# Last products through six PSUM accumulators, and modulation units moved to the ends of mixers and norms

## Chip, cores and metric

One Trainium2 chip, of which the kernel uses one core. The metric is the device time of one execution in microseconds (us). TensorE is called PE, VectorE DVE, ScalarE ACT, GpSimd POOL; SP issues nearly all DMAs, in order.

## What is computed

Two transformer blocks in a row on 256 latent tokens of width 1024, with 256 context tokens beside them, all in float32. The first block has two layers. Each splits one projection into three mixers, joins their outputs in one product, and has a feed-forward with a convolution; the context goes through layer 0 as well, but not through the end of layer 1. Every sum into x is gated by a modulation vector, which is itself a product of the condition c with a large weight:

```python
sh1, sc1, g1, sh2, sc2, g2 = modulation(c, w_ada[i], b_ada[i])
h = modulate(rms_norm(x, norm1_g[i]), sh1, sc1)
a_z, bq, bk, bv, cq, ck, cv = split_proj(h @ w_in[i])
...
x = x + g1 * (jnp.concatenate([out_a, out_b, out_c], axis=-1) @ w_out[i])
x = x + g2 * conv_ffn(modulate(rms_norm(x, norm2_g[i]), sh2, sc2),
                      w_up[i], conv_w[i], conv_b[i], w_down[i])
```

out_a is a gated MLP over positions, out_b windowed attention with grouped heads and a sink, out_c differential attention whose result gets a norm of its own. The second block has one layer with full attention and one with a pooling mixer, each with such a feed-forward.

## The kernel before

**Products.** A float32 product is made of three faster ones. `mms` issues them: high part by high part (L285), low part of the activations by high part of the weights or the like (L286), high by low (L289). The weights come through a staging tile `w`; ACT casts the high half (wh, L238) and DVE subtracts for the low half (wl, L240). Activations are cast on ACT (hH, mixH, gH) and their rest made on DVE or POOL (hL, mixL, gL). One product of 256 columns over four tiles of 128 rows is 12 matmuls.

**PSUM.** The products named `acc` use two buffers of one bank, transposes and small sums `tr` two, scores and the feed-forwards' `up` products `S` two buffers of two banks each. Where a buffer is free only when DVE or ACT has read it, PE waits.

**Order.** The orders of PE and SP are those of the code. Those of ACT, DVE and POOL are set by a scheduler. The class `Line` runs the pieces of work as generators: each yields a cost and a waiting time (table WAIT), and `Line` goes on with a piece when its estimated due time has come, so pieces are interleaved on PE's order. `spread(main, fill)` puts the elements of one list evenly between those of another.

**Mixer.** `block1` builds the list `seq`: the chunks of the projection (c0 to c7 of the latent and context stream), the score groups of the three mixers (`b_unit`: scores on PE at L807 with a mask at L810, maximum on DVE at L661, exponentials on ACT at L817; `c_unit`: the like, with products L873 and L881 for its own norm and a cast to mixH at L266), and the first half of the output product, `wouts(0)`. In layer 1 a table of four moves, `MOVES`, then takes elements at given places of `seq` to other places, counted modulo its length. Behind `seq` come, stream by stream, the last eight output products, `wouts(1)` (`wout`, residual at L980, sums of squares, and the norm's products at L485 and L486).

**Feed-forward.** `ffn` makes `up` products, and `down` products in groups; those of the last group stand at its end, eight per stream, each with its residual (L980) or, in the second block, its sum into y (L1051). Behind them come the next norm (var, rstd, and per tile ht at L529 and hL at L540) and the next layer's first chunk.

**Modulation units.** A unit loads a piece of the modulation weight (`mod_load`, on SP: `mw` in two halves through three buffers, or `wm` of 1 MB through the larger pool x8), multiplies (L410), adds up on ACT or DVE (L414, L416) and now and then transposes (L426). Each unit loads for the next one. `fill_a` gives layer 0 its 16 pieces, 12 elements between the scores and five between the first output products; layer 1 has eight pieces spread over `seq` from its twelfth element on.

Of the kernel before, what the change touches and what calls it, by code (L numbers as in the profile page):

```python
# [19 lines left out]
P = 128  # L20
# [59 lines left out]
def spread(main, fill):  # L80

    out, done = [], 0
    for i, u in enumerate(main):
        out.append(u)
        want = len(fill) * (i + 1) // len(main)
        out += fill[done:want]
        done = want
    return out + fill[done:]
# [17 lines left out]
class Stack:  # L106
# [191 lines left out]

    def psum(self, tag, shape):
        return self.ps.tile(shape, F32, tag=tag, name=tag)  # L300

    def x8(self, name, dt=F32):
        return self.xp.tile([P, CH], dt, tag="x8", name=name)
# [402 lines left out]
    def block1(self, l, after):  # L706
# [12 lines left out]
        u, gk = uv[:, 0], f"gn{l}"  # L719
# [5 lines left out]
        def mix_tiles(g):  # L725
            if g not in mix:
                if f"wout{l}" in WHOLE:
                    t = self.gp.tile([P, CH], F32, tag="gH", name="mix") if g == 0 else self.x8("mix")
                    mix[g] = (t.rearrange("p (k t) -> p k t", k=4),)
                elif g == 0:  # L730
                    mix[g] = (self.gp.tile([P, 4, 512], F32R, tag="gH", name="mixH"),
                              self.gp.tile([P, 4, 512], F32R, tag="gL", name="mixL"))
                else:
                    mix[g] = tuple(self.x8(t, F32R).rearrange("p (k t) -> p k t", k=4) for t in ("mixH", "mixL"))
            return mix[g]

        def chunk(ci, post, ss):
            return [lambda s=s: self.go(self.proj(f"win{l}", ci, s, post), f"c{ci}{s}") for s in ss]
# [6 lines left out]
        def post_bq(c):  # L745
            return lambda acc, s: self.qk(acc, 4, 64, tbq, self.sm(gk, "bq"), s == 0, rsB[:, s, :, c], 2,
                                          qTB[:, s, 2 * c:2 * c + 2])
# [142 lines left out]
        def wout(g, cc, f4, c):  # L890

            m = mix_tiles(g)
            w = self.weights(f"wout{l}", 2 * g + cc, k=4)
            ft = 4 * cc + f4
            acc = self.psum("acc", [P, 512])
            fs = slice(P * f4, P * f4 + P)
            yield from self.mms([acc[:, c]], range(4), lambda b, k: [x[:, k, fs] for x in w],
                     lambda b, k: [x[:, k, c] for x in m])
            self.residual(l, 2, acc, ft, [q for q in streams if c.start <= 256 * q < c.stop])
            if g == 1:  # L900
                self.sumsq(nst[c.start // 256], self.xs[c.start // 256][:, ft], ft == KD - 1)

        def wouts(g, c):
            return [lambda cc=cc, f4=f4: self.go(wout(g, cc, f4, c)) for cc in range(2) for f4 in range(4)]
# [18 lines left out]
        need = lambda *names: [lambda: line.ensure(*names)]  # L923
        rev = streams[::-1]
        fill = self.fill_a(l)
        seq = chunk(0, post_bkv, (0,)) + chunk(1, post_bq(0), (0,)) + chunk(0, post_bkv, (1,))
        if l == 0:
            seq += chunk(1, post_bq(0), (1,))
        else:
            seq = seq[:2] + need("n1") + [self.last_loads] + seq[2:]  # L930
        self.qk_wait = WAIT[f"qk{l}_first"]
        seq += [lambda: setattr(self, "qk_wait", WAIT[f"qk{l}"])]
        heavy = (chunk(2, post_bq(1), streams) + chunk(3, post_ck, both) + chunk(4, post_cq, streams)
# [18 lines left out]
        for a, b in MOVES[l]:  # L952
            seq.insert((a + b) % len(seq), seq.pop(a % len(seq)))
        if l == 1:
            seq = seq[:12] + spread(seq[12:], self.more_units((1, 12, 20)))
        for u_ in seq:
            u_()
        if l == 1:
# [1 line left out]
            self.ctx2_h()  # L960
        for q in streams:
            line.ensure(*(f"c_{hp}{q}11" for hp in range(2)))
            for u_ in wouts(1, slice(256 * q, 256 * q + 256)):
                u_()
            line.due()
            self.go(self.norm_h(l, 3, self.sm(key, "n2g"), nst[q], q), f"n{q}")
# [29 lines left out]
    def ffn(self, i, T, streams, after):  # L996


        nc, key = self.nc, f"sm{i}"
        post = i >= 2  # L1000
        groups = FF_GROUPS[T]
        starts = [sum(groups[:g]) for g in range(len(groups))]
        nst = {q: {} for q in streams}
        y = self.x8("y").rearrange("p (k t) -> p k t", k=KD) if post else None
        gt = {}
        cols = 512 if T == 512 else 256

        def up(g, j):
            a = j - starts[g]
            if a == 0:  # L1010
                gt[g] = tuple(self.gp.tile([P, groups[g], T], F32R, tag=t, name=t) for t in ("gH", "gL"))
            wh, wl = self.weights(f"wup{i}", j, k=KD)
            ps = self.psum("S", [P, 2, 512])
            for q in streams:
                hH, hL = self.h[q]
                yield from self.mms([ps[:, b, 256 * q:256 * q + 256] for b in range(2)], range(KD),
                         lambda b, k: (wh[:, k, P * b:P * b + P], wl[:, k, P * b:P * b + P]),
                         lambda b, k: (hH[:, k], hL[:, k]))
            c = self.pt.tile([P, 2, 512], F32, tag="pt", name="cgv")
            self.conv(c[:, 0, :T], ps[:, 0, :T], key, j)  # L1020
            nc.scalar.activation(c[:, 0, :T], c[:, 0, :T], AF.Silu)
            if i < 2:
                self.conv(c[:, 1, :T], ps[:, 1, :T], key, KF + j)
                nc.vector.tensor_tensor(c[:, 1, :T], c[:, 0, :T], c[:, 1, :T], ALU.mult)
            else:
                nc.vector.tensor_tensor(c[:, 1, :T], c[:, 0, :T], ps[:, 1, :T], ALU.mult)
            gH, gL = gt[g]
            nc.scalar.copy(gH[:, a], c[:, 1, :T])  # L1028
            (nc.vector if T == 512 else nc.gpsimd).tensor_tensor(gL[:, a], c[:, 1, :T], gH[:, a].bitcast(F32), ALU.subtract)  # L1029
            if j == KF - 1:  # L1030
                self.lnexp()

        def down(g, ft, c):
            gk = groups[g]
            cc, f4 = divmod(ft, cols // P)
            wh, wl = self.weights(f"wdn{i}", g, cc, k=gk)
            gH, gL = gt[g]
            fs = slice(P * f4, P * f4 + P)
            acc = self.psum("acc", [P, 512])
            yield from self.mms([acc[:, c]], range(gk), lambda b, k: (wh[:, k, fs], wl[:, k, fs]),  # L1040
                     lambda b, k: (gH[:, k, c], gL[:, k, c]))
            last = g == len(groups) - 1
            if not post:
                self.residual(i, 5, acc, ft, [q for q in streams if c.start <= 256 * q < c.stop])
                if last:
                    self.sumsq(nst[c.start // 256], self.xs[c.start // 256][:, ft], ft == KD - 1)
            else:
                if g == 0:
                    nc.scalar.copy(y[:, ft], acc[:, :256])
                else:  # L1050
                    nc.vector.tensor_tensor(y[:, ft], y[:, ft], acc[:, :256], ALU.add)  # L1051
                if last:
                    self.post_sums(nst[0], y[:, ft], ft, i == 3)

        main = []
        for kind, g, j in self.ffn_order(T):
            if kind == "up":
                main.append(lambda g=g, j=j: self.go(up(g, j)))
            elif g < len(groups) - 1:
                main += [lambda g=g, ft=ft: self.go(down(g, ft, slice(0, T))) for ft in range(KD)]  # L1060
        for u in spread(main, self.fill_f(i)):
            u()
        if i == 0:
            self.prep1(1)
        if post:
            nst[0] = self.post_start(i, 5, self.sm(key, "post2"))
        for q in streams:
            for ft in range(KD):
                self.go(down(len(groups) - 1, ft, slice(256 * q, 256 * q + 256)))
                if i == 2:  # L1070
                    self.early_loads(ft)
            after(q, nst[q], y)
# [260 lines left out]
    def fill_a(self, l):  # L1333

        if l:
            return [], []
        u = self.more_units((0, 8, 24))
        return u[:12], u[12:]

    def fill_f(self, i):  # L1340

# [78 lines left out]
    def first(self, S, wh, wl, pr, s):  # L1420
        mm = self.nc.tensor.matmul
        hH, hL = self.h[s]
        for k in (2 * pr, 2 * pr + 1):
            for t in range(2):
                o, ts = S[:, t, :256], slice(P * t, P * t + P)
                mm(o, lhsT=hH[:, k, ts], rhs=wh[:, k], start=k == 0, stop=False)
                mm(o, lhsT=hH[:, k, ts], rhs=wl[:, k], start=False, stop=False)
                mm(o, lhsT=hL[:, k, ts], rhs=wh[:, k], start=False, stop=k == KD - 1)
# [197 lines left out]
```

## Time and profile before

| | us |
|---|---|
| median of three runs | 1756.46 |
| the runs | 1751.83, 1756.46, 1756.65 |
| the profiled execution's own time | 1754.48 |
| its span, first to last instruction | 1752.7 |
| PE busy in it | 1599.5 |
| DVE busy in it | 1188.5 |

PE's mean granted clock is 0.967 of full speed. In the profile an instruction's line is that of the kernel; `out<-in` are the tiles. A wait is the idle time of an engine before an instruction, with what released it. The places by time: layer 0's first output products lie from 205 to 266 us, the last ones up to 312; the first feed-forward ends at 741, where layer 1 begins; its mixer goes on to 920; the third feed-forward ends near 1490.

### The profile page before, as it was taken

Reading aid. Unit: us, or ns where it says so; the run is one execution under the profiler, and the core shown is the slowest. Engines: PE = TensorE matmul, PEld = TensorE weight load, DVE = VectorE, ACT = ScalarE, POOL = GpSimd, SP = SyncE. Lnnn points to the kernel's source line nnn. Section 1 sums busy time; section 2 is a strip of 40 time slices with the busy share of each in tenths; the row PEclk is TensorE's granted clock in tenths of the full one; section 3 lists DMA queues with packets and bytes.
Section 4 is the critical chain, followed back from the end, with each engine's and each line's share of the span. In section 5 each row is a group of like instructions: output and inputs, shape, how many; then the busy total and the mean of one; then the engine's idle time right before and its main releaser. Section 6 shows DMA issues by size and latency. Waiting matters only on the chain.

```text
span 1752.7 us, 32334 instructions
## 1 busy us (share of the span) xinstructions
PE 1599.5 (91%) x12604; PEld 1419.1 (81%) x12604; DVE 1188.5 (68%) x2877; ACT 879.1 (50%) x2147; POOL 136.7 (8%) x162
## 2 busy tenths in 40 slices
PE   6999797999999999889888998988979999779997
PEld 5877457989898989788468998976869999479996
DVE  5765886755555545777788777785776567876665
ACT  6344654523242324455546656563556555656563
POOL 1000001000000000010000101000141012330110
PEclk9999998999999999999899999999989999889999
DMA  8344330444545454334334544565554546435552
GB/s 326 107 145 145 125 125 32 146 182 177 219 143 217 168 205 176 131 119 154 133 109 151 195 167 139 175 220 208 197 180 164 196 155 226 174 118 196 170 176 88
DMA packets 67402, 288.36 MB, mean 165 GB/s; under 512 B 7728, under 2 KB 9008, under 8 KB 54960
## 3 DMA queue, kind: packets, MB, share of 16 engines
q1 hardware_dynamic: 65664, 283.91, 46.0%
q10 hardware_dynamic: 1584, 2.38, 0.4%
q8 instruction: 99, 1.62, 0.4%
q14 instruction: 55, 0.45, 0.1%
HBM read 285.21 MB, written 1.05 MB: 163 GB/s over the span
## 4 chain that ended last, share of the span: by engine, by line
PE 61%; DVE 18%; DMA 10%; ACT 7%; issue 3%; POOL 1%; SPq 0%; ACTq 0%; DVEq 0%; POOLq 0%
PE S L285 9%; PE S L286 9%; PE S L289 9%; PE acc L285 8%; PE acc L286 8%; PE acc L289 8%; DVE wl L240 6%; DMA w<-in_wup_dram 5%; PE acc L410 3%; ACT wh L238 2%; DMA w<-in_wdn_dram 2%; DVE ht L529 1%; PE tr L671 1%; DMA wm<-in_wmod_dram 1%; DVE mx L661 1%
## 5 line engine op out<-in xcount | busy, mean ns | idle before, releaser
L240 DVE TENSOR_TENSOR wl<-w,wh 128x384 fp32r<-128x384 f32 (+2 forms) x1010 | 489.1, 523 | 218.5 <-ACT wh L238 190.7
L238 ACT CAST wh<-w 128x384 fp32r<-128x384 f32 (+2 forms) x1010 | 421.3, 475 | 329.4 <-DMA w<-in_wup_dram 94.9
L285 PE MATMUL S<-hH,wh 128*128 128x256 f32 x1408 | 351.3, 287 | 31.0 <-ACT hH L539 17.4
L286 PE MATMUL S<-hL,wh 128*128 128x256 f32 x1408 | 349.2, 285 | 4.7 <-POOL hL L537 4.0
L285 PEld LDWEIGHTS S<-hH,wh 128*128 128x128 f32 x1408 | 271.6, 193 | 36.9 <-ACT hH L539 18.1
L286 PEld LDWEIGHTS S<-hL,wh 128*128 128x128 f32 x1408 | 271.5, 193 | 7.1 <-POOL hL L537 5.0
L285 PE MATMUL acc<-gH,wh 128*128 128x256 f32 (+1 forms) x728 | 209.0, 311 | 9.2 <-DVE xc L980 4.8
L286 PE MATMUL acc<-gL,wh 128*128 128x256 f32 (+1 forms) x728 | 205.3, 306 | 0.0
L289 PE MATMUL S<-hH,wl 128*128 128x256 f32 x1408 | 198.4, 284 | 0.0
L289 PEld LDWEIGHTS S<-hH,wl 128*128 128x128 f32 x1408 | 182.6, 193 | 0.0
L285 PEld LDWEIGHTS acc<-gH,wh 128*128 128x128 f32 x728 | 138.9, 191 | 23.6 <-issue 7.0
L289 PE MATMUL acc<-gH,wl 128*128 128x256 f32 (+1 forms) x728 | 145.7, 306 | 0.0
L286 PEld LDWEIGHTS acc<-gL,wh 128*128 128x128 f32 x728 | 138.9, 191 | 5.5
L991 DVE SCALAR_TENSOR_TENSOR cgv<-S,sm,cgv 128x255 f32<-128x255 f32 (+1 forms) x132 | 74.8, 567 | 67.6 <-ACT cgv L988 67.1
L289 PEld LDWEIGHTS acc<-gH,wl 128*128 128x128 f32 x728 | 110.2, 191 | 6.5
L988 ACT ACTIVATE cgv<-S,sm 128x256 f32<-128x256 f32 (+1 forms) x132 | 82.7, 628 | 47.3 <-PE S L289 47.3
L285 PE MATMUL acc<-wh,hH 128*128 128x256 f32 x344 | 91.2, 296 | 10.4 <-ACT hH L539 8.2
L1029 POOL TENSOR_TENSOR gL<-cgv,gH 128x256 fp32r<-128x256 f32 x66 | 52.2, 791 | 579.5 <-ACT gH L1028 558.7
L980 DVE SCALAR_TENSOR_TENSOR x<-acc,mod,x 128x256 f32<-128x256 f32 x104 | 50.0, 482 | 57.7 <-PE acc L289 57.3
L286 PE MATMUL acc<-wl,hH 128*128 128x256 f32 x344 | 88.1, 287 | 0.0
L286 PE MATMUL S<-hcL,wh 128*128 128x256 f32 x352 | 86.5, 284 | 0.3 <-DVE hcL L540 0.3
L285 PE MATMUL S<-hcH,wh 128*128 128x256 f32 x352 | 86.4, 280 | 0.0
(268 smaller groups left out, 2837.4 us busy)
## 6 DMA issues: line engine op xcount, KB each, us to landing
wm<-in_wmod_dram SPq DMA_DIRECT2D x72, 1024.0 KB, 7.6
w<-in_wup_dram SPq DMA_DIRECT2D x140, 512.0 KB, 3.9
w<-in_wdn_dram SPq DMA_DIRECT2D x56, 512.0 KB, 4.1
mw<-in_wmod_dram SPq DMA_DIRECT2D x48, 512.0 KB, 4.7
w<-in_wup_dram SPq DMA_DIRECT2D x18, 1024.0 KB, 7.5
w<-in_win_dram SPq DMA_DIRECT2D x32, 512.0 KB, 4.0
w<-in_wout_dram SPq DMA_DIRECT2D x16, 512.0 KB, 4.7
w<-in_wqkv_dram SPq DMA_DIRECT2D x16, 512.0 KB, 3.9
```

The lines of the kernel that those rows point to most:

```text
L238: self.nc.scalar.copy(h[:, c:d], w[:, c - a:d - a])
L240: self.nc.vector.tensor_tensor(l[:, c:d], w[:, c - a:d - a], h[:, c:d].bitcast(F32), ALU.subtract)
L285: mm(o, lhsT=s[0], rhs=m[0], start=k == ks[0], stop=False)
L286: mm(o, lhsT=s[0], rhs=m[1], start=False, stop=False)
L289: mm(o, lhsT=S(b, k)[1], rhs=M(b, k)[0], start=False, stop=end and k == ks[-1])
L410: nc.tensor.matmul(acc[32 * u:32 * u + 32], lhsT=self.cpad[:, k], rhs=w[:, 256 * u:256 * u + 256], start=k == ks[0], stop=k == ks[-1])
L529: nc.vector.scalar_tensor_tensor(t, self.xs[s][:, ft], A, r, ALU.mult, ALU.mult)
L661: nc.vector.tensor_reduce(mx, S[:, :, :nk], AX.X, ALU.max)
L980: self.nc.vector.scalar_tensor_tensor(x, acc[:, c], self.mods(i, j)[:, ft, s:s + 1], x, ALU.mult, ALU.add)
L988: nc.scalar.activation(out, ps, AF.Identity, scale=cw[:, n + f:n + f + 1], bias=cb[:, f:f + 1])
L991: nc.vector.scalar_tensor_tensor(o[:, :, 1:256], x[:, :, 0:255], cw[:, f:f + 1], o[:, :, 1:256], ALU.mult, ALU.add)
L1029: (nc.vector if T == 512 else nc.gpsimd).tensor_tensor(gL[:, a], c[:, 1, :T], gH[:, a].bitcast(F32), ALU.subtract)
```

## The change

Four things are changed. (1) `last_acc` gives the last output products of `block1` and the last `down` products of all four feed-forwards an accumulator: products 0, 1, 4, 5 of eight take `acc` as before, 2 and 3 the two halves of one S buffer, 6 and 7 those of the next. (2) In layer 0 four of the sixteen units (n = 20 to 23) are no longer among the first output products; they are kept, and run ahead of products 0 and 4 of each stream's last eight. (3) In layer 1 the first two of eight units (n = 12, 13) are loaded at the end of the first feed-forward, through x8, and run as one unit (`pair1`) early in `seq`; four are spread from the thirteenth element on; two (n = 18, 19) are kept and run ahead of products 0 and 4. (4) `pair1` lengthens `seq` by one, ahead of the places that `MOVES` names, and `MOVES` is as before. So its four moves take other elements: the pair itself goes three places on, behind `last_loads` (the load of the context for layer 1) and a chunk, and `last_loads`, which went three places on, stays; the score group that went one place ahead is b100, the first of the second pair of heads.

```diff
+    def last_acc(self, ft):
+
+
+        if ft // 2 % 2 == 0:
+            return self.psum("acc", [P, 512])
+        if ft % 2 == 0:
+            self.S2 = self.psum("S", [P, 2, 512])
+        return self.S2[:, ft % 2]
...
-            acc = self.psum("acc", [P, 512])
+            acc = self.last_acc(ft) if g == 1 else self.psum("acc", [P, 512])
...
-            seq = seq[:2] + need("n1") + [self.last_loads] + seq[2:]
+            seq = seq[:2] + self.pair1 + need("n1") + [self.last_loads] + seq[2:]
...
         for a, b in MOVES[l]:
             seq.insert((a + b) % len(seq), seq.pop(a % len(seq)))
         if l == 1:
-            seq = seq[:12] + spread(seq[12:], self.more_units((1, 12, 20)))
+            fill = self.more_units((1, 14, 20))
+            self.kept = fill[5:]
+            seq = seq[:13] + spread(seq[13:], fill[:5])
...
-            for u_ in wouts(1, slice(256 * q, 256 * q + 256)):
+            for ft, u_ in enumerate(wouts(1, slice(256 * q, 256 * q + 256))):
+                if ft in (0, 4) and self.kept:
+                    self.kept.pop(0)()
                 u_()
...
-            acc = self.psum("acc", [P, 512])
+            last = g == len(groups) - 1
+            acc = self.last_acc(ft) if last else self.psum("acc", [P, 512])
...
         if i == 0:
             self.prep1(1)
+            first, *self.pair1 = self.more_units((1, 12, 14), x8=True, m=2)
+            first()
...
         u = self.more_units((0, 8, 24))
-        return u[:12], u[12:]
+        self.kept = u[13:]
+        return u[:12], u[12:13]
```

The order of the instructions shows three places. Line numbers of the changed kernel are higher by 9 up to `wout`, and by 13 at the residual (L993 there is L980 here).

The first is PE's order at the end of layer 0's mixer, from the last tile's norm product (`tr<-ocsq`), whose result becomes the last mixH, to the next norm's products (`tr<-nacc`, `tr<-sq`). Before:

```order
L881 MATMUL tr<-ocsq,cst 128x256
L285 MATMUL acc<-mixH,wh 128x256
L286 MATMUL acc<-mixL,wh 128x256
L285 MATMUL acc<-mixH,wh 128x256
L286 MATMUL acc<-mixL,wh 128x256
L289 MATMUL acc<-mixH,wl 128x256 x2
L485 MATMUL tr<-nacc,ones 128x256
L486 MATMUL tr<-sq,ones 128x256
```

Now:

```order
L890 MATMUL tr<-ocsq,cst 128x256
L285 MATMUL S<-mixH,wh 128x256
L286 MATMUL S<-mixL,wh 128x256
L285 MATMUL S<-mixH,wh 128x256
L286 MATMUL S<-mixL,wh 128x256
L289 MATMUL S<-mixH,wl 128x256 x2
L285 MATMUL S<-mixH,wh 128x256
L286 MATMUL S<-mixL,wh 128x256
L285 MATMUL S<-mixH,wh 128x256
L286 MATMUL S<-mixL,wh 128x256
L289 MATMUL S<-mixH,wl 128x256 x2
```

Six matmuls stood between the two before, the third of which wants the last mixH. Now there are 24 and a kept unit: 18 on S, of which the first ten rows are shown and five more of the same kind follow, the unit (L419, 8 matmuls), and the old six.

The second is DVE's order at the end of the first feed-forward, among the norm's rows (ht, hL) and the residuals of the context (xc). Before:

```order
L503 TENSOR_TENSOR var<-var,rstd 128x256
L980 SCALAR_TENSOR_TENSOR xc<-acc,mod_108,xc 128x256
L504 SCALAR_TENSOR_TENSOR rstd<-var,rstd 128x256
L529 SCALAR_TENSOR_TENSOR ht<-x,mscale,rstd 128x256 x3
L540 SCALAR_TENSOR_TENSOR hL<-ht,mod_109,hH 128x256 x3
L529 SCALAR_TENSOR_TENSOR ht<-x,mscale,rstd 128x256 x3
L540 SCALAR_TENSOR_TENSOR hL<-ht,mod_109,hH 128x256 x3
L529 SCALAR_TENSOR_TENSOR ht<-x,mscale,rstd 128x256 x2
L980 SCALAR_TENSOR_TENSOR xc<-acc,mod_108,xc 128x256
L540 SCALAR_TENSOR_TENSOR hL<-ht,mod_109,hH 128x256 x2
L477 TENSOR_TENSOR nacc<-nacc,sq 128x256
L980 SCALAR_TENSOR_TENSOR xc<-acc,mod_108,xc 128x256
```

Now:

```order
L993 SCALAR_TENSOR_TENSOR xc<-S,mod_108,xc 128x256
L512 TENSOR_TENSOR var<-var,rstd 128x256
L513 SCALAR_TENSOR_TENSOR rstd<-var,rstd 128x256
L538 SCALAR_TENSOR_TENSOR ht<-x,mscale,rstd 128x256 x3
L549 SCALAR_TENSOR_TENSOR hL<-ht,mod_109,hH 128x256 x3
L538 SCALAR_TENSOR_TENSOR ht<-x,mscale,rstd 128x256 x3
L549 SCALAR_TENSOR_TENSOR hL<-ht,mod_109,hH 128x256 x3
L538 SCALAR_TENSOR_TENSOR ht<-x,mscale,rstd 128x256 x2
L993 SCALAR_TENSOR_TENSOR xc<-S,mod_108,xc 128x256
L549 SCALAR_TENSOR_TENSOR hL<-ht,mod_109,hH 128x256 x2
L486 TENSOR_TENSOR nacc<-nacc,sq 128x256
L993 SCALAR_TENSOR_TENSOR xc<-acc,mod_108,xc 128x256
```

One residual fewer stands ahead of the ht rows; the fourth, of an S half, is now behind them, and the fifth, which frees the `acc` buffer of product 4, comes after one more hL row and a sum of squares.

The third is PE's order in layer 1's mixer, at the scores of the b mixer (S<-kvqc, and the mask S<-msk). Before, from the first group on:

```order
L620 MATMUL tr<-cst,rp_8336 128x128 x4
L807 MATMUL S<-kvqc,qTB 128x512 x2
L810 LDWEIGHTS identb
L810 MATMUL S<-msk,identb 128x128
L810 LDWEIGHTS identb
L810 MATMUL S<-msk,identb 128x128
L807 MATMUL S<-kvqc,qTB 128x512 x2
L810 LDWEIGHTS identb
L810 MATMUL S<-msk,identb 128x128
L810 LDWEIGHTS identb
L810 MATMUL S<-msk,identb 128x128
L285 MATMUL acc<-wh,hH 128x256
```

Now, from the second group on:

```order
L816 MATMUL S<-kvqc,qTB 128x512 x2
L819 LDWEIGHTS identb
L819 MATMUL S<-msk,identb 128x128
L819 LDWEIGHTS identb
L819 MATMUL S<-msk,identb 128x128
L816 MATMUL S<-kvqc,qTB 128x512 x2
L819 LDWEIGHTS identb
L819 MATMUL S<-msk,identb 128x128
L819 LDWEIGHTS identb
L819 MATMUL S<-msk,identb 128x128
L629 MATMUL tr<-cst,rp_8427 128x128 x4
L285 MATMUL acc<-wh,hH 128x256
```

Before, a chunk's product on `acc` followed the second group. Now a third group stands there, and a transposition of the next group's query.

On SP's queue, in layer 0, two of the `wout` loads stand ahead of four more halves of modulation loads than before, and the last four such halves stand between the feed-forward's first `wup` loads.

## Rows read from the trace of the kernel before

**Rows 1.** The page, parts 1 and 4: busy times; the chain by engine.

```profile
PE 1599.5 (91%) x12604; PEld 1419.1 (81%) x12604; DVE 1188.5 (68%) x2877; ACT 879.1 (50%) x2147; POOL 136.7 (8%) x162
...
PE 61%; DVE 18%; DMA 10%; ACT 7%; issue 3%; POOL 1%; SPq 0%; ACTq 0%; DVEq 0%; POOLq 0%
```

**Rows 2.** PE's waits: what waited for what, us in total, times, longest.

```profile
PE acc L285 <- ACT mixH L266: 9.2, 3, 3.6
...
PE acc L285 <- DVE xc L980: 7.6, 2, 4.8
...
PE acc L285 <- DVE y L1051: 2.0, 4, 0.6
```

**Rows 3.** PE, end of layer 0: start, us, instruction, [idle before, releaser].

```profile
270.10 0.58 PE L285 MATMUL acc<-mixH,wh 128*128 128x256 f32 x1 [2.75 <-ACT mixH L266]
...
290.55 0.58 PE L285 MATMUL acc<-mixH,wh 128*128 128x256 f32 x1 [3.65 <-ACT mixH L266]
...
303.07 0.39 PE L285 MATMUL acc<-mixH,wh 128*128 128x256 f32 x1 [2.81 <-DVE xc L980]
```

**Rows 4.** Windows: us, busy PE, PEld, DVE, ACT, POOL; granted clock, DMA share, GB/s.

```profile
205.00:266.00 61.00, 55.45 (x326) 33.53 (x326) 53.04 (x142) 31.47 (x87) 0.00 (x0) 0.97 0.30 95
270.00:275.00 5.00, 4.90 (x22) 4.73 (x23) 2.56 (x8) 0.46 (x2) 0.00 (x0) 0.50 0.68 209
275.00:280.00 5.00, 5.00 (x38) 5.00 (x38) 2.59 (x6) 1.00 (x3) 0.00 (x0) 0.85 0.01 4
290.00:295.00 5.00, 4.45 (x15) 3.92 (x16) 1.06 (x4) 1.29 (x3) 0.00 (x0) 0.52 0.00 0
295.00:300.00 5.00, 5.00 (x37) 5.00 (x35) 4.25 (x11) 2.05 (x5) 0.00 (x0) 0.80 0.00 0
735.00:740.00 5.00, 2.62 (x12) 2.62 (x13) 4.89 (x13) 3.33 (x9) 0.00 (x0) 0.73 0.00 0
800.00:840.00 40.00, 40.00 (x317) 31.70 (x316) 26.28 (x74) 23.73 (x57) 0.00 (x0) 1.00 0.47 152
```

**Rows 5.** Timeline of PE, then of DVE, end of the first feed-forward.

```profile
737.38 0.58 PE L285 MATMUL acc<-gH,wh 128*128 128x256 f32 x1 [4.83 <-DVE xc L980]
...
741.12 0.28 PE L285 MATMUL acc<-wh,hH 128*128 128x256 f32 x1
741.24 0.28 PE L286 MATMUL acc<-wl,hH 128*128 128x256 f32 x1
...
736.84 0.48 DVE L980 SCALAR_TENSOR_TENSOR xc<-acc,mod,xc 128x256 f32<-128x256 f32 x1
...
738.36 0.49 DVE L980 SCALAR_TENSOR_TENSOR xc<-acc,mod,xc 128x256 f32<-128x256 f32 x1
```

**Rows 6.** PE's timeline, one modulation unit.

```profile
902.00 1.07 PE L410 MATMUL acc<-mw,cpad 128*32 128x256 f32 x16
```

**Rows 7.** SP's queue: when each DMA issue begins, and how long it took.

```profile
197.29 37.66 SPq L372 DMA_DIRECT2D mw<-in_wmod_dram  x4
...
709.15 1.00 SPq L224 DMA_DIRECT2D w<-in_win_dram  x2
```

**Rows 8.** PE, then DVE, last mixer tile and norm, layer 0.

```profile
286.07 0.60 PE L881 MATMUL tr<-ocsq,cst 128*128 128x256 f32 x2
...
305.41 0.48 DVE L980 SCALAR_TENSOR_TENSOR xc<-acc,mod,xc 128x256 f32<-128x256 f32 x1 [1.61 <-PE acc L289]
```

**Rows 9.** Timeline of PE, then of ACT, layer 1's mixer.

```profile
785.06 1.04 PE L620 MATMUL tr<-cst,rp 128*128 128x128 f32 x4 [1.91 <-DVE rp L649]
...
789.50 0.28 PE L810 MATMUL S<-msk,identb 128*128 128x128 bf16 x2
...
792.20 0.66 PE L620 MATMUL tr<-cst,rp 128*128 128x128 f32 x4 [0.93 <-DVE rp L649]
...
846.40 1.10 PE L849 MATMUL S<-kvc,kvqc 32*128 32x512 f32 x2 [2.83 <-ACT Pm L817]
...
793.17 0.77 ACT L817 ACTIVATE Pm<-S,nm,rsB 128x512 f32<-128x512 f32 x1
```

More of the change, by code (lines that the diff above doesn't have):

```diff
@@ L1038, in down @@
             fs = slice(P * f4, P * f4 + P)
-            acc = self.psum("acc", [P, 512])
+            last = g == len(groups) - 1
+            acc = self.last_acc(ft) if last else self.psum("acc", [P, 512])
             yield from self.mms([acc[:, c]], range(gk), lambda b, k: (wh[:, k, fs], wl[:, k, fs]),
                      lambda b, k: (gH[:, k, c], gL[:, k, c]))
-            last = g == len(groups) - 1
             if not post:
```

## Prediction

> **What bounds the kernel now.** I read the page first. TensorE (PE) is busy for 91% of the span, VectorE (DVE) for 68%, and PE holds 61% of the chain that ended last, DVE 18% [rows 1]. So time can come from two places: PE work that disappears, of which there is none here, and PE's idle time, which is 1752.7 - 1599.5 = 153 us. The list of PE's waits says which part of it the change can reach: waits for the mixers' last tile (mixH), for a residual sum on DVE (xc L980), and for the y sums of the last feed-forwards (y L1051) [rows 2]. Then I went to each place in the timeline. At the end of layer 0's mixer PE stands still for 2.75, 3.65 and 2.81 us, the first two until ScalarE (ACT) has cast mixH, the third until DVE has emptied one of two `acc` buffers [rows 3]. Around these gaps the granted clock reads 0.50 and 0.52, the 1.2 GHz level nearly alone, and 0.80 to 0.85 in the 5 us after [rows 4]. At the end of the first feed-forward one gap of 4.83 us waits for a residual [rows 5]. In layer 1's mixer I read when S buffers come free [rows 9].
>
> **The sum** is made against the profiled execution's 1754.48 us, which lies 2.0 us under the median of the runs.
>
> *Layer 0, the middle.* Four of the five modulation units that stood among the first eight output products (`wout`) go to the tail. One takes 1.07 us of PE [rows 6]; 4 x 1.07 = 4.28 us leave a stretch of 61.0 us in which PE is busy for 55.45 and DVE for 53.04 [rows 4]. PE's queue is thus 5.55 us from full and DVE's 8.0. The change also moves two wout loads ahead of modulation loads: they sat behind one whose issue took 37.66 us on SP's queue [rows 7]. The ends are 0 (PE's waits there grow by what it no longer does) and -4.3; PE is nearer to full than DVE, so I take half, **-2.1**.
>
> *Layer 0, the end.* The kept units run before products 0 and 4 of each stream. The one at product 0 of the first stream lies in the 2.75 us gap, the one at product 0 of the second in the 3.65 us gap; the two at product 4 lie on the path, 2 x 1.07 = **+2.1**. The 3.65 us gap: its chain runs from the norm's product (L881, at 286.07) over DVE and ACT to mixH, with which PE goes on at 290.55: 4.5 us that nothing in the change shortens [rows 3, 8]. But the order puts L881 18 matmuls further ahead of the one that wants mixH, and a matmul takes 0.12 us at the full clock: two in a row start at 741.12 and 741.24 [rows 5]. So 18 x 0.12 = 2.2 us more work covers the chain, beside the kept unit: **-2.2** (ends 0 and -3.65). The 2.81 us gap: PE needs `acc` while DVE stands in the norm's ht and hL rows. With six accumulators product ft takes the buffer of ft-4 or of the other pair, whose residuals are two or more products old: **-2.8** (ends 0 and -2.8). It can turn up again as a wait for DVE at L485; DVE itself waited for PE there for 1.61 us [rows 8], so it has room, and I take the whole. The clock: the 20 us windows named read 0.50, 0.85, 0.52 and 0.80; at full clock their PE work of 19.35 us would have been 2.5 + 0.75 + 2.4 + 1.0 = 6.6 us shorter at most [rows 4]. One of the two dips hangs on the 3.65 us gap, 3.4 us; as the chain is bridged with almost nothing to spare I take **-1.5** (ends 0 and -5). Together -4.4. Six `wup` loads now stand behind the last kept units' loads on SP's queue. The kept loads wait for the units' own matmuls, all of them ahead of the feed-forward on PE, so I price them at 0; if that cover were gone, the feed-forward's first products would wait for a load and a split.
>
> *End of the first feed-forward.* PE stops at 732.55 (737.38 - 4.83) after the context's product 5 and resumes at 737.38 when DVE's residual at 736.84 is through; it does two products at a reduced clock and begins layer 1 at 741.12 [rows 5]. After the change the two products need no wait; then layer 1's first product wants an `acc` buffer. By the order its residual stands one place behind the residual that ends the gap now, at about 738.4 [rows 5]. So layer 1 begins at best 2.7 us earlier, and the wait stays as a gap of some 3.7 us with its slow clock behind it. Ends 0 and -2.7; I take **-2.0**, since less of the slow clock falls on the old products. Two modulation loads more stand ahead of the first `win` load, which is issued at 709.15 now while its product starts at 741.12 [rows 5, 7]: 32 us of cover, so 0.
>
> *Layer 1.* The list of moves names places in a sequence that is one element longer, so other elements move: the third score group of the b mixer now follows the first two at once on PE. It needs a third S buffer and there are two. The first is free when ACT has done its exponentials, at 793.94; PE is through with the second group at 789.78 [rows 9]. So PE stands 4.1 us; what it does now in that time it does afterwards, without the 0.93 us gap at 792.20, which has passed by then [rows 9]: **+3.2** (ends 0, if ACT gets there sooner since the context load and its squares now come earlier, and +4.1). A gap of this size is followed by the slow clock elsewhere [rows 3, 4]: **+1.5** (0 to +2.4). Two units run early, 2 x 1.07 us [rows 6], before a gap of 1.91 us in which PE waits for DVE's rp [rows 9]: between 0 and +2.1, and I take 0, since the gap holds them. Four of eight units leave the later stretch, -4.3 at most, but PE has gaps there, as the 2.83 us at 846.40 [rows 9], that would only grow: half, **-2.2**, and one unit is on the path at product 4: **+1.1**. The scores being earlier, such gaps may shrink: one of them, **-2.6** (ends 0 and -5). Layer 1 together **+1.0**, between -6 and +8.
>
> *The other last products.* y sums of the last but one feed-forward: four waits, 2.0 us together [rows 2]. The norm behind them wants the last y sum from the same DVE, so I take a third, **-0.7** (0 to -2.0). The list has no such wait for the other two feed-forwards [rows 2]: 0.
>
> Sum: -2.1 - 4.4 - 2.0 + 1.0 - 0.7 = -8.2; 1754.5 - 8.2 = **1746.3 us**.
>
> **Rivals.** *The extra buffers give nothing.* DVE is the real bound of both tails: the 2.81 and 4.83 us gaps come back before L485 and layer 1's first product. For it: DVE is busy for 4.89 of the 5 us around the end of the second gap [rows 4]. Against it: DVE waits for PE at 305.41 [rows 8]. Then the terms -2.8, -1.5, -2.0 and -0.7 go and -2.1 + 2.1 - 2.2 + 1.0 = -1.2 is left: 1753.3. The Trainium skill's page TensorE: Matmul & The Clock Gate, section HAM oscillation - how this bites in real kernels, tells of a kernel in which double-buffering PSUM brought nothing once the order of the work was mended; by it the buffers would be worth zero here too and the sum would be this rival's. The 2.81 us row, where PE waits for a buffer and DVE soon after for PE, speaks against it.
>
> *Slower.* The third score group stalls PE for 4.1 us, the slow clock costs 2.4, the two groups behind it (b101, b200) meet the same two buffers, half the price again (+3.2), the pair lies on the path (+2.1), the product-4 unit too (+1.1), and nothing leaves the later stretch: layer 1 +12.9. With the middle of layer 0 at 0, its end at -2.2 + 2.1, and nothing else, 1754.5 + 12.8 = 1767. It decides if the exponentials of the second group end after PE has nothing left beside them. For it: two S buffers, three groups. Against it: from 800 to 840 PE is never idle [rows 4], so there is work to put behind.
>
> *More.* The clock stays at its upper level through the filled gaps. The tail of layer 0 then gives 5 instead of 1.5, the first feed-forward's end 2.7 and 1.3 of clock (0.73 over 5 us [rows 4]), and layer 1 comes out at -2: 1754.5 - 2.1 - 7.9 - 4.0 - 2.0 - 0.7 = 1738. The Trainium skill's page TensorE: Matmul & The Clock Gate, section A second HAM failure mode: psum-queue depth-cycling, says that PE idling between groups while it cycles through PSUM makes the clock swing; by it a deeper rotation would end the swings, which gives this rival's time. The dips here stand behind mixH waits as well [rows 3], which no buffer removes.
>
> **How the numbers follow.** Forecast 0.55, buffers worth nothing 0.20, slower 0.12, more 0.13. A measurement of this kernel tells about 0.3%, 5.3 us, from no change, so faster is under 1751.2 and slower over 1761.7. Faster: 0.13 and most of 0.55, less what its own spread (1740 to 1753) puts over the line: 0.64. Same: that rest and the buffers worth nothing, 0.24. Slower: 0.12. The range goes from 1737 (more) to 1757 (the upper part of worthless buffers); the slower case and a little below are left out.
>
> **What would show it.** Right: no PE wait for L980 at the end of layer 0, the gap before the second stream's products under 1.5 us, clock above 0.6 behind it; layer 1 beginning about 8.5 us earlier (6.5 + 2); a new PE wait of about 4 us for an S buffer in layer 1, before the third score group. Wrong: the same microseconds standing before L485; PE's share of the 205 to 266 stretch falling without the stretch getting shorter; or layer 1 longer by over 5 us.

## Result and the profile after

| | us |
|---|---|
| before, median of six runs | 1754.14 (1750.42 to 1757.23) |
| after, median of six runs | 1773.66 (1766.79 to 1787.97) |
| ratio, 95% interval | 1.0108 (1.0079 to 1.0137) |
| span of the profiled execution, after | 1786.2 |

The change makes the kernel 1.1% slower, some 19 us; I had forecast 8 us less. Ratios, here and below, are taken over all executions and can differ by 0.1% from the quotient of the medians. The profiled execution of after is the longest of its six, so single stretches of it are not to be read as the median's. What PE waits for is to be read from it. PE's list of waits, after (what waited for what, us in total, times, longest):

```profile
PE S L285 <- DVE xc L993: 10.7, 4, 5.3
...
PE acc L419 <- DMA mw<-in_wmod_dram: 9.2, 5, 3.3
...
PE S L285 <- DVE x L993: 8.5, 8, 2.6
...
PE S L285 <- DVE y L1064: 8.1, 4, 4.3
...
PE S L816 <- ACT Pm L826: 5.2, 1, 5.2
...
PE tr L792 <- issue: 4.1, 1, 4.1
...
PE acc L285 <- DVE x L993: 2.0, 1, 2.0
```

Lines are those of the changed kernel: L993 and L1064 are the residual and the y sum, L980 and L1051 before; L419 is a modulation unit (L410), L816 the b scores (L807). The waits for mixH [rows 2] are gone. The waits for DVE's residuals and y sums were to shrink. They stand at 10.7 + 8.5 + 8.1 + 2.0 = 29.3 us, against 7.6 + 2.0 us [rows 2] and 1.7 us for x before, and nearly all of them are of products on S, the new accumulators. There are 16 of these: two for each of the eight sequences of last products (two streams in layer 0 and in the first feed-forward, one in layer 1, one in each of the three others).

Where in a sequence they stand, PE's timeline shows at the end of the first feed-forward, after. The columns are start, duration, instruction and, in brackets, the idle time before it and its releaser:

```profile
744.02 0.28 PE L289 MATMUL acc<-gH,wl 128*128 128x256 f32 x1
744.14 0.28 PE L285 MATMUL S<-gH,wh 128*128 128x256 f32 x1
...
745.10 0.28 PE L289 MATMUL S<-gH,wl 128*128 128x256 f32 x1
750.64 0.58 PE L285 MATMUL S<-gH,wh 128*128 128x256 f32 x1 [5.26 <-DVE xc L993]
```

DVE's timeline, the residuals of the same stretch:

```profile
747.13 0.48 DVE L993 SCALAR_TENSOR_TENSOR xc<-S,mod,xc 128x256 f32<-128x256 f32 x1
...
748.65 0.48 DVE L993 SCALAR_TENSOR_TENSOR xc<-acc,mod,xc 128x256 f32<-128x256 f32 x1
...
749.38 0.48 DVE L993 SCALAR_TENSOR_TENSOR xc<-acc,mod,xc 128x256 f32<-128x256 f32 x1
...
750.11 0.48 DVE L993 SCALAR_TENSOR_TENSOR xc<-S,mod,xc 128x256 f32<-128x256 f32 x1
```

From 744.14 PE makes product 6, nine matmuls into the first half of an S tile. Product 7 goes to the second half, which nobody uses. Yet it starts only when DVE is through with the residual of product 6, which reads the first half, at 750.11 + 0.48, and that is the fourth of four residuals in DVE's queue. With two `acc` buffers product 7 had waited for the residual of 5; now it waits for that of 6. This reads as if the halves of an S tile were handled as one buffer, so that a write to one waits for the reads of the other; e1 and e3 below test it.

At the end of layer 0's mixer the clock did what I forecast at one place of three. The mixer's end lies some 8 us later in this execution, so windows are to be compared by place and not by time. The product that waited for mixH at 290.55 before [rows 3] stands near 298 here, and there the clock reads 1.00 where it read 0.52 and 0.80 [rows 4]. Behind the two other places, which have a gap again, it reads 0.68 (from 280) and 0.71 (from 305). Windows of after, with span, busy PE, PEld, DVE, ACT and POOL, granted clock, DMA share and GB/s:

```profile
280.00:285.00 5.00, 5.00 (x32) 5.00 (x31) 1.82 (x7) 1.64 (x5) 0.00 (x0) 0.68 0.87 343
295.00:300.00 5.00, 4.59 (x41) 3.77 (x42) 3.50 (x10) 1.33 (x4) 0.00 (x0) 1.00 0.43 150
300.00:305.00 5.00, 3.46 (x29) 3.25 (x28) 4.48 (x12) 2.76 (x7) 0.00 (x0) 1.00 0.06 24
305.00:310.00 5.00, 2.50 (x11) 2.50 (x12) 3.62 (x7) 4.30 (x13) 3.55 (x5) 0.71 0.00 0
```

PE's timeline, after: three further gaps.

```profile
278.16 0.64 PE L419 MATMUL acc<-mw,cpad 128*32 128x256 f32 x8 [3.27 <-DMA mw<-in_wmod_dram]
...
307.50 0.58 PE L285 MATMUL S<-mixH,wh 128*128 128x256 f32 x1 [4.04 <-DVE xc L993]
...
806.29 1.22 PE L816 MATMUL S<-kvqc,qTB 64*128 64x512 f32 x2 [5.16 <-ACT Pm L826]
```

The first kept unit waits 3.27 us for the second half of its own load, in the place of 2.75 us for mixH [rows 3]. The gap at 303.07 [rows 3] is back with 4.04 us, this time for the half. The third group of b scores waits 5.16 us for an S buffer, and the gated MLP's first products (L792) stand 4.1 us for a cause that the list doesn't name.

### The profile page after: what moved, and what is told of

Its sections match the earlier page's. It is cut to its first block, busy times and chain, and to the rows that moved or that the text cites. A ratio compares the mean times of both kernels' runs of the same rounds, so it can differ in the third digit from the quotient of the medians.

```text
span 1786.2 us, 32299 instructions
## 1 busy us (share of the span) xinstructions
PE 1618.3 (91%) x12604; PEld 1430.3 (80%) x12604; DVE 1188.3 (67%) x2876; ACT 879.2 (49%) x2147; POOL 132.9 (7%) x162
## 4 chain that ended last, share of the span: by engine, by line
PE 61%; DVE 18%; DMA 10%; ACT 7%; issue 3%; POOL 0%; SPq 0%; ACTq 0%; DVEq 0%; POOLq 0%
PE S L285 10%; PE S L286 9%; PE S L289 9%; PE acc L285 8%; PE acc L286 7%; PE acc L289 7%; DVE wl L240 6%; DMA w<-in_wup_dram 5%; PE acc L419 3%; ACT wh L238 2%; DMA w<-in_wdn_dram 2%; DVE ht L538 2%; PE tr L680 2%; DVE mx L670 1%; DMA wm<-in_wmod_dram 1%
## 5 line engine op out<-in xcount | busy, mean ns | idle before, releaser
L285 PE MATMUL acc<-gH,wh 128*128 128x256 f32 (+1 forms) x620 | 180.4, 314 | 3.3 <-DVE x L993 2.0
L286 PE MATMUL acc<-gL,wh 128*128 128x256 f32 (+1 forms) x620 | 177.6, 310 | 0.0
L285 PEld LDWEIGHTS acc<-gH,wh 128*128 128x128 f32 x620 | 118.1, 191 | 16.3 <-issue 7.2
L289 PE MATMUL acc<-gH,wl 128*128 128x256 f32 (+1 forms) x620 | 125.8, 309 | 0.0
L286 PEld LDWEIGHTS acc<-gL,wh 128*128 128x128 f32 x620 | 118.2, 191 | 5.5
L289 PEld LDWEIGHTS acc<-gH,wl 128*128 128x128 f32 x620 | 93.9, 190 | 6.5
L1041 ACT CAST gH<-cgv 128x256 fp32r<-128x256 f32 (+1 forms) x88 | 40.4, 459 | 88.4 <-DVE cgv L1037 66.2
```

Of the source, the lines that this page charges most:

```text
L285: mm(o, lhsT=s[0], rhs=m[0], start=k == ks[0], stop=False)
L286: mm(o, lhsT=s[0], rhs=m[1], start=False, stop=False)
L289: mm(o, lhsT=S(b, k)[1], rhs=M(b, k)[0], start=False, stop=end and k == ks[-1])
```

## Experiments

Twelve kernels ran, in three groups of four; each group had its own runs of the kernel before on its chip. Ratios are to these.

**e1, the halves alone.** The changed kernel without its moved units.

```diff
         u = self.more_units((0, 8, 24))
-        self.kept = u[13:]
-        return u[:12], u[12:13]
+        self.kept = []
+        return u[:12], u[12:]
...
-            seq = seq[:2] + self.pair1 + need("n1") + [self.last_loads] + seq[2:]
+            seq = seq[:2] + need("n1") + [self.last_loads] + seq[2:]
...
-            fill = self.more_units((1, 14, 20))
-            self.kept = fill[5:]
-            seq = seq[:13] + spread(seq[13:], fill[:5])
+            seq = seq[:12] + spread(seq[12:], self.more_units((1, 12, 20)))
...
-            first, *self.pair1 = self.more_units((1, 12, 14), x8=True, m=2)
-            first()
```

> The kernel before with the accumulators of the change alone (products 2, 3 and 6, 7 of the last eight in the two halves of one S buffer), no unit moved. Theory H (the second half of an S tile is only written when DVE has read the first, so PE stops after products 2 and 6 of every last eight): nearly all of the loss is here, 12 to 18 us over before, 1766 to 1772, with PE waits on x, xc and y for S products of some 20 us together where before has 11. Rival M (the loss comes from the moved units and the shifted list of moves in layer 1): 2 to 6 us faster than before, as I forecast for the buffers alone, 1748 to 1752.

Ratio 1.0079 (1.0053 to 1.0106), 1773.75 against 1757.71 us. PE's list of waits, e1:

```profile
PE S L285 <- DVE xc L991: 10.2, 4, 5.3
...
PE S L285 <- DVE x L991: 7.0, 7, 2.8
...
PE S L285 <- DVE y L1062: 5.4, 4, 1.7
```

22.6 us on S, as H expects; with 1.8 us on `acc` that is 13 us more than before's 11.3, about the loss. M falls for the greater part of the loss.

**e2, the units without the halves.**

```diff
     def last_acc(self, ft):
-        if ft // 2 % 2 == 0:
-            return self.psum("acc", [P, 512])
-        if ft % 2 == 0:
-            self.S2 = self.psum("S", [P, 2, 512])
-        return self.S2[:, ft % 2]
+        return self.psum("acc", [P, 512])
```

> The change without its accumulators: all last products on acc as before, units moved in both layers, list of moves shifted as in the change. H: within 5 us of before, 1749 to 1759. M: 12 to 20 us over before, 1766 to 1774, nearly all of it between 741 and 921 us, in layer 1's mixer.

Ratio 1.0024 (1.0007 to 1.0041). H holds, but the units are no gain either. The next groups look for why.

**e3, the halves four products apart.** e1 with the same two S tiles and the same four halves, dealt out in another order:

```diff
-        if ft % 2 == 0:
-            self.S2 = self.psum("S", [P, 2, 512])
-        return self.S2[:, ft % 2]
+        if ft < 4:
+            self.S2 = (self.S2 if ft == 3 else []) + [self.psum("S", [P, 2, 512])]
+        return self.S2[ft % 2][:, ft // 4]
```

> As e1, but the halves are dealt out so that the two halves of one S tile are four products apart: product 2 takes the first half of one tile, 3 the first of another, 6 and 7 their second halves. The same six accumulators. H: the waits after products 2 and 6 vanish, PE's waits on residuals fall under 6 us together, and the time is 3 to 7 us under before, 1747 to 1751. M: the same as e1. Rival D (DVE is the bound of the tails, the place of the wait does not matter): within 2 us of before, 1752 to 1756, with the wait at the norms' products.

Ratio 0.9960 (0.9941 to 0.9979), 1751.97 us. From the list of e3's waits:

```profile
PE acc L285 <- DVE x L991: 1.9, 1, 1.9
...
PE acc L285 <- DVE y L1062: 0.4, 1, 0.4
```

No last product on S waits for DVE any more, and the only difference to e1 is which products share a tile: 1.2% between the two. That settles H: products that share a tile wait for each other's reads. Whether the program's bookkeeping or the chip joins the two halves, these runs do not separate. D falls by the time, 7 us under before where it allowed 2, but not by the place: at the end of layer 0 PE now stands 2.77 us before the norm's product, about as long as in the 2.81 us gap [rows 3], as D and the rival of worthless buffers had said. What is left of the 4.83 us gap [rows 5] stands where I had put it, before layer 1's first product, but for another reason and shorter. PE's timeline, e3:

```profile
313.75 0.70 PE L494 MATMUL tr<-nacc,ones 128*128 128x256 f32 x2 [2.77 <-DVE nacc L486]
...
738.73 0.55 PE L285 MATMUL acc<-wh,hH 128*128 128x256 f32 x1 [2.75 <-ACT hH L548]
```

Most of the gain lies behind that: from the last norm's products of layer 0's mixer (`tr<-nacc`) to layer 1's first product e3 takes 425.0 us (313.75 to 738.73), before 430.1 (311.02 to 741.12).

**e4, the whole change with the halves apart** (e3's edit in the changed kernel).

> The whole change with its halves four products apart as in e3. H: what I forecast for the change with six free accumulators, 1743 to 1752. M: 1766 to 1774, as the change. D: 1752 to 1758.

Ratio 0.9995 (0.9975 to 1.0016), 1756.08 us: no gain, and in the range of D, which e3 had ruled out by the time. Beside e3 this says that the moved units take back what the mended accumulators give.

**e5, layer 0's units alone.** The kernel before with `self.kept = u[13:]` and the two lines in front of the last products; layer 1 as before.

> Only layer 0's part of the moved units; all products on acc, layer 1 as before. Theory U1 (of the units, layer 1's part with its shifted moves costs, layer 0's part gains): 2 to 6 us under before; from the first output product to the first norm 76 us instead of 80 to 81. Rival U0 (keeping units costs wherever it is done, since they stand on the path): 2 to 5 us over before.

Ratio 0.9961 (0.9940 to 0.9981). From the first output product to the first norm it takes 75.8 us (216.75 to 292.53) where before takes 81.0; the six other profiles that leave layer 0's units in their places (e1, e3, e6, e9, e10, e11) take 78.9 to 82.3. U1 holds.

**e6, layer 1's units alone, with the moves counted one higher.**

```diff
-MOVES = ((), ((15, 4), (49, 3), (25, 3), (14, -1)))
+MOVES = ((), ((16, 4), (4, 3), (26, 3), (15, -1)))
```

> Only layer 1's part of the moved units, with each place in the list of moves one higher, so that the moves take the elements they took before. Theory S (the shifted moves cost layer 1 its 5 to 6 us): the 5.2 us wait for a third S buffer and the 4 us gap before the gated MLP's products are gone, layer 1's mixer (first b scores to its last norm) is at 133 to 138 us as before instead of 145, and the time within 4 us of before. Rival P (the early pair and the kept units cost it): mixer at 142 us or more and 4 to 8 us over before.

Ratio 1.0054 (1.0034 to 1.0074). The wait for a third S buffer is gone (of the gap before the gated MLP 3.0 us are left), but the time is up by 9 us, where S allowed 4. So S falls: the shifted moves are not what layer 1's part costs in the main. P's direction holds. The mixer takes 139.2 us (796.92 to 936.09), between the two theories, and decides nothing: profiles in which layer 1's units and moves are as before take 135.3 (before) to 139.5 us (e3).

**e7, e3 and e5 together.**

> Halves four products apart, with layer 0's part of the units alone. If the gains add up, -0.4% of the accumulators and U1's 2 to 6 us: 6 to 12 us under before, ratio 0.993 to 0.997. If the two are the same microseconds (both fill the same gaps): as the accumulators alone, 0.996.

Ratio 0.9944 (0.9918 to 0.9970), 1746.99 us. Alone the two give 0.40% and 0.39%, together 0.56%: they add up in part.

**e8, the whole change with both mended** (e3's accumulators, e6's moves).

> The whole change with both suspected faults mended: halves four products apart, moves counted one higher. S: 6 to 12 us under before, ratio 0.993 to 0.997, no wait for a third S buffer in layer 1. P: no better than 0.998.

Ratio 0.9995 (0.9976 to 1.0014), the same as e4, whose moves are shifted. S falls again.

**e9, the shift alone.** The kernel before with an empty element where the pair was put.

```diff
-            seq = seq[:2] + need("n1") + [self.last_loads] + seq[2:]
+            seq = seq[:2] + [lambda: None] + need("n1") + [self.last_loads] + seq[2:]
...
-            seq = seq[:12] + spread(seq[12:], self.more_units((1, 12, 20)))
+            seq = seq[:13] + spread(seq[13:], self.more_units((1, 12, 20)))
```

> The kernel before, with an empty element in the list of layer 1's mixer at the place where the change puts its pair; no unit moved, accumulators as before. So only the four moves take other elements. Theory S2 (the shift costs about 3 us: the third score group waits 5.2 us for an S buffer, part of which other gaps give back): ratio 1.000 to 1.003, the wait for S there. Rival (the shift costs its full 5 us and a 4 us gap before the gated MLP): 1.004 to 1.006.

Ratio 1.0012 (0.9990 to 1.0033): not told from nothing, within S2's bounds. Its wait stands alone in PE's timeline, e9:

```profile
796.44 1.22 PE L812 MATMUL S<-kvqc,qTB 64*128 64x512 f32 x2 [5.16 <-ACT Pm L822]
```

The gap before the gated MLP is at most 0.6 us here and in e10 and e11. It is 4.1 to 4.3 us in after, e2 and e4, and 3.0 us in e6 and e8, so it is seen only where the pair and the kept units are together; its cause stays open.

**e10, the early pair alone.** Before, with the pair's two lines at the end of the first feed-forward, `self.pair1` in `seq`, the other six units spread as before, and e6's moves.

> The kernel before, with the first two of layer 1's units loaded at the end of the first feed-forward and run as an early pair; moves counted one higher, nothing kept, accumulators as before. Theory L (the two 1 MB loads push the first weight load of layer 1 back, DVE's splits of it come into the residuals of the feed-forward's end, and the pair stands behind a gap and not in it): 4 to 6 us over before, ratio 1.002 to 1.004, with a PE wait of 2 us for x residuals before 741 us that before does not have. Rival K (the kept units cost it): within 1 us of before.

Ratio 1.0028 (1.0006 to 1.0050). SP's queue, e10 (start and length of a group of issues):

```profile
710.63 9.44 SPq L371 DMA_DIRECT2D wm<-in_wmod_dram  x4
720.50 11.94 SPq L224 DMA_DIRECT2D w<-in_win_dram  x4
```

ACT's timeline, before, with the cast of the first `win` load, its first user:

```profile
715.91 1.24 ACT L238 CAST wh<-w 128x384 fp32r<-128x384 f32 x3 [6.58 <-DMA w<-in_win_dram]
```

DVE's timeline, e10:

```profile
730.73 1.35 DVE L240 TENSOR_TENSOR wl<-w,wh 128x384 fp32r<-128x384 f32 x3
...
732.00 0.87 DVE L987 SCALAR_TENSOR_TENSOR x<-acc,mod,x 128x256 f32<-128x256 f32 x2
```

PE's timeline, e10:

```profile
732.53 0.58 PE L285 MATMUL acc<-gH,wh 128*128 128x256 f32 x1 [2.03 <-DVE x L987]
...
766.18 3.26 PE L415 MATMUL acc<-wm,cpad 128*32 128x256 f32 x32 [3.60 <-ACT wh L238]
```

With two more modulation loads in it the group holds SP's queue for 9.44 us, so the first `win` load is issued 9.9 us behind them; before, 4.4 us lay between (704.71 and 709.15, [rows 7]). Before, its casts start at 715.91 and its splits end at 722.0, one or two at a time between the residuals, and PE has no such wait. In e10 the splits come as two runs of three, from 729.12 on, with residuals behind them, and PE waits 2.03 us for one. The pair stands behind the 3.6 us gap and not in it, and takes 3.26 us of PE. L holds on both counts.

**e11, layer 1's kept units alone.**

```diff
-            seq = seq[:12] + spread(seq[12:], self.more_units((1, 12, 20)))
+            fill = self.more_units((1, 12, 20))
+            self.kept = fill[7:]
+            seq = seq[:12] + spread(seq[12:], fill[:7])
```

> The kernel before, with the last two of layer 1's units run ahead of products 0 and 4 of the last eight; no pair, moves as before, accumulators as before. K: 3 to 6 us over before, ratio 1.002 to 1.004, with a wait of 2 to 3 us for the kept unit's own load in place of the 2.75 us for mixH, and a second unit on the path. L: within 2 us of before.

Ratio 1.0014 (0.9995 to 1.0032), not told from nothing and, at 2.5 us, between K and L: the time decides for neither. K's wait is there. PE's timeline, e11:

```profile
905.44 0.64 PE L415 MATMUL acc<-mw,cpad 128*32 128x256 f32 x8 [2.53 <-DMA mw<-in_wmod_dram]
...
910.24 0.39 PE L285 MATMUL acc<-mixH,wh 128*128 128x256 f32 x1 [2.54 <-DVE msum L421]
```

The unit waits for its load, and a product behind it waits for the unit's sum on DVE.

**e12, the best version: e7 with the first kept unit's load given time.** The unit that stood directly ahead of the first kept one, and held the buffers its load needs, goes to the middle of the first eight output products.

```diff
-        seq += cc[:2] + need(*bnames) + spread(cc[2:], spread(w0, fill[1]))
+        seq += cc[:2] + need(*bnames) + spread(cc[2:], w0[:3] + fill[1] + w0[3:])
```

> As e7, with the unit that stands directly ahead of the first kept one moved to the middle of the first eight output products, so that the kept unit's load has some 25 us and not one unit's time. If the load is what the kept unit waits for (3.1 us in e8): that wait gone, 1 to 2 us under e7, ratio 0.992 to 0.995. If the chain to mixH sets that place anyway: as e7, the wait named mixH again.

Ratio 0.9931 (0.9905 to 0.9957), 1742.11 against 1756.18 us. The same place in PE's timeline, first e7:

```profile
271.43 0.64 PE L419 MATMUL acc<-mw,cpad 128*32 128x256 f32 x8 [3.41 <-DMA mw<-in_wmod_dram]
```

and e12:

```profile
269.45 1.07 PE L419 MATMUL acc<-mw,cpad 128*32 128x256 f32 x16
271.01 0.39 PE L285 MATMUL acc<-mixH,wh 128*128 128x256 f32 x1 [0.49 <-ACT msum L423]
```

The windows from 270 to 275 us, e7:

```profile
270.00:275.00 5.00, 3.57 (x24) 3.15 (x25) 1.19 (x6) 0.37 (x1) 0.00 (x0) 0.77 0.91 311
```

and e12:

```profile
270.00:275.00 5.00, 4.51 (x45) 4.03 (x38) 2.64 (x7) 0.87 (x3) 0.00 (x0) 1.00 0.68 247
```

Both mixH gaps of layer 0 are gone, and every window of 5 us from 265 to 320 reads a granted clock of 1.00. e12 beats the kernel before by 0.7% and the changed one by 1.8 points. The intervals of e12 and e7 overlap, so that e12 is better than e7 is likely from the trace, not shown by the times.

## Why the prediction was wrong

Measured one by one, against before: the halves +0.79%, layer 0's units -0.39%, the shift +0.12%, the pair +0.28%, layer 1's kept units +0.14%; together +0.94%, where the whole change measures +1.08%. Each part is known to about 0.2%, so within that the parts account for the loss; that they simply add is not shown (e7 gave less than its two parts, and e8 no gain where its parts add up to -0.37%).

- **The step that failed** is the sentence on six accumulators: "product ft takes the buffer of ft-4 or of the other pair, whose residuals are two or more products old". Products 3 and 7 share a tile with the product before them, and wait for a residual that has only just been asked for. The terms that rested on it, -2.8, -2.0, -0.7 and part of the -1.5, were to give about 6 us; e1 shows +14 us (0.79% of 1757.7) in their place. The mechanism was sound with buffers that are free: e3 gives -7 us (4 to 10 by its interval). The sizes of its places were off. The 2.81 us gap, priced at -2.8, came back as a wait of 2.77 us before the norm's product, one of my own signs of being wrong; the stretch up to there is still 1 to 5 us shorter (from the first output product 96.3 us in e3, 97.3 to 101.4 in before, e6, e9, e10 and e11). The first feed-forward's end, priced at -2.0, comes out 4 to 5 us shorter with free buffers (425.0 us in e3, 426.0 in e7, 426.5 in e12, against 430.1 before). I had counted buffers by the names in the instructions' order, where nothing tells that a product waits.
- **Layer 0's units**: -2.1 + 2.1 - 2.2 and a share of the -1.5, so some -3; e5 gives -7 us (3 to 11 by its interval). The sign and the place were right: the 3.65 us gap [rows 3] is gone and the clock behind it is up. Which term was too small the runs do not settle. From the first output product to the first stream's last norm product (`tr<-ocsq`) e5 takes 49.5 us against 53.6 before, 4.1 less where I had taken 2.1; but other runs with these units moved take up to 52.0 (after). That the unit ahead of the path waits for its own load I had not seen: I placed it in the 2.75 us gap, and e7 and e12 show that the gap became its load's.
- **The first feed-forward's end**: I priced the later `win` load at 0, with 32 us to layer 1's first product as its cover. The cover was measured to the wrong user. ACT and DVE take that load up long before, 25 us ahead of the product (715.91 and 741.12 in before), and DVE in a queue that holds the residuals too, and PE waited 2.03 us there (e10).
- **Layer 1**, with its loads at the first feed-forward's end: +1.0 forecast, between -6 and +8; e6 and the difference of e2 and e5 (0.24% + 0.39%) give 9 to 11 us. The wait of the third score group was right in kind and place, 5.16 us for my 4.1; but its net price is small, +0.12%, not to be told from 0 (e9), where I had +4.7. The pair, which I priced at 0 as lying in a gap of DVE's, is the dearest of these at +0.28% (0.06 to 0.50). The kept units are at +0.14% for my -2.2 + 1.1, not to be told from 0.
- **The rivals.** The slower rival had the sign, by another mechanism: it blamed the score groups. None of them held that a second half waits for the first. The rival of worthless buffers was right that the waits come back before the norm and before layer 1's first product (2.77 and 2.75 us in e3), but falls by the time: buffers that are free are worth 0.4% here. The Trainium skill's page TensorE: Matmul & The Clock Gate, section HAM oscillation - how this bites in real kernels, told of no gain from double-buffering in its kernel. This case's e3, with six accumulators for two, does gain (0.9960). "The clock stays up" came true in part, in e12, when the gaps were really filled. Buffers alone do not do it: in e3 both mixH waits stand as before, 2.75 and 3.65 us, and the clock reads 0.50 in the window from 295, behind the second.
- **My signs.** Of those for right, three came. The gap before the second stream's products is gone (what is left, 0.76 us at 295.41, stands before an S half), the clock behind it reads 1.00, and the wait before the third score group is there (5.16 us). Two failed: a wait for the residuals stands at the end of layer 0 (4.04 us), and layer 1 begins 2.9 us later and not 8.5 earlier, counted from the first output product (219.54 to 752.73, before 210.86 to 741.12). With free halves, in e4, it begins 7.7 us earlier (213.68 to 736.20). So up to layer 1 the forecast of 8.5 us holds about in size once the buffers are free, as far as single executions tell. One sign for wrong came: layer 1 is longer by over 5 us, 192.2 us from its first product to its mixer's norm (752.73 to 944.90), against 180.2 (before) to 187.3 (e3) where its units and moves are as before.
- **The scale.** The forecast rested on an execution at the lower end. The stretch up to layer 0's first output product, in which nothing that PE does was changed, took 210.9 us there and 211.1 to 219.5 us in the thirteen others that I read. That shifts the level of the forecast and not its difference to before. The clock's bound of 6.6 us was taken over whole windows; over the PE work in them it is 6.3, which changes no term.

## To carry over

In this kernel two accumulators in one tile, a bank each, were ordered as one buffer: deal them out so that products which share a tile are as far apart as possible, and read the waits, not the tile names, before counting buffers. A load that is moved must be followed to its first user on every engine, the cast on ACT and the split on DVE, and not only to the product. A unit put into a gap has to have its load done by then, or the gap becomes its own.

## What I had not expected of the hardware

Two executions whose PE instructions are the same up to 205 us differ by 6.6 us there (210.86 and 217.48 us to the first output product). They are 1.9 us apart at 191.38 and 193.30, at the same product (`tr<-ut,wsT`); the other 4.7 us come behind it. The windows of before:

```profile
195.00:205.00 10.00, 7.87 (x50) 4.61 (x52) 8.33 (x23) 5.64 (x15) 0.00 (x0) 1.00 0.30 107
```

and of e3:

```profile
195.00:205.00 10.00, 8.64 (x31) 5.36 (x31) 6.36 (x19) 1.53 (x4) 0.00 (x0) 0.50 0.42 155
```

The clock was granted at 2.4 GHz in the one and at 1.2 GHz in the other, after a row of small PE gaps, 0.2 to 1.9 us each, that is nearly the same in both. What decides between the two levels there these rows don't tell. Single executions of this kernel differ by it as much as most parts of this change are worth.
